# Where the selection's bias is added to the sparse attention scores: on TensorE or on VectorE

## The chip, the cores and the metric

The kernel runs on one core of a Trainium2 chip. A core has five engines that work side by side, each through its own queue in order: TensorE (PE in the profile, its weight loads PEld), VectorE (DVE), ScalarE (ACT), GpSimd (POOL) and SyncE (SP), which here issues the transfers. Matrix products land in PSUM, eight banks of 128 x 512 floats; everything else lives in SBUF. The metric is the device time of one execution in microseconds (us), smaller being better; the time given is the median of the runs.

## What is computed

One block of a streaming encoder over 256 frames of width 1024: a norm, one projection, two attention branches (A: latent attention, B: sparse attention), their gated merge, a projection, and then a mixture of 32 experts. The change touches branch B alone. For every query it scores all admissible keys with a small indexer, keeps the best 64, and attends to those only:

```python
logits = jnp.einsum('bqhd,bkd->bqhk', qii, k_idx).astype(jnp.float32) * (IDX_DIM ** -0.5)
score = jnp.einsum('bqh,bqhk->bqk', wi.astype(jnp.float32), jax.nn.relu(logits))
score = jnp.where(adm[None], score, -jnp.inf)
_, sel = lax.top_k(score, top_k)
sel_ok = (sel // CHUNK) <= q_chunk[None, :, None]
k_sel = gather(k, sel)
v_sel = gather(v, sel)
s = jnp.einsum('bqhd,bqkhd->bhqk', qi, k_sel).astype(jnp.float32) * (DSA_HEAD_DIM ** -0.5)
s = jnp.where(sel_ok[:, None], s, NEG)
p = jax.nn.softmax(s, axis=-1).astype(v.dtype)
return jnp.einsum('bhqk,bqkhd->bqhd', p, v_sel)
```

There are 8 heads of 64 channels, and the 256 queries are two blocks of 128.

## The kernel before, in words

The kernel gathers nothing. `select(j)` (lines 477 to 499) works out the indexer's scores of query block `j`, marks the 64 largest of each row, and writes `bias`, a table of 128 queries by 128 (`j`=0) or 256 (`j`=1) keys: 0 at a chosen key and -1e30 elsewhere (line 499). The attention then runs over all keys of the block, with that bias added to the scores before the softmax, so that keys that are not chosen get weight zero.

`attend_pairs(quad, ...)` (lines 610 to 664) does this for four heads, as a generator that is stepped by hand (lines 727 to 731): first both query blocks of quad 0, then both of quad 1, then the two closing steps. One *round* is one query block `j` of one quad; there are four. A round takes two PSUM banks `p[0]`, `p[1]` from a pool of two (`pss`), two heads in each. It then does, in this order:

- on TensorE, for each bank, one product of the identity with `bias` that opens the bank's sum (line 621, 256 columns for `j`=0 and 512 for `j`=1, full array);
- on TensorE, twelve products of queries and keys (`mm3_pair`, line 318): 32-bit numbers are split into a high and a low part, so each score takes three products, and the two banks use the two halves of the array's rows in turn. They add onto the bias;
- on VectorE, per bank, the negated maximum of each row and head (line 632), read from PSUM;
- on ScalarE, per head, the exponential of scores plus that number with its row sum (line 638), read from PSUM and written to the SBUF tile `P`;
- on VectorE the reciprocal of the sums and the scaling of `P` (lines 641, 643);
- on TensorE the transposes of `P` (line 649), on ScalarE their copy to `PT` (lines 651, 653).

After a quad's two rounds, 16 products with the values (line 661) and a split of the result into high and low (lines 291, 294) give `obT`. It is an operand of the third group of output projections.

Work around it. `project_late` (lines 734 to 746) multiplies the normed input with the gates' weights and the attention results with their output weights. Each 128 x 512 piece of weight is split by `split_late` into a high part on ScalarE (line 282, or 297 where a gain is applied) and a low part on VectorE (line 283, or 297), into four buffers `halves` used in turn, and then feeds six products of 512 columns on TensorE (`mm3`, lines 301 to 303). These pieces need nothing from the sparse attention until `obT`, and TensorE works on them between the steps of the rounds; on ScalarE and VectorE the splits stand in the same queues as the rounds' work. The order on each engine is fixed when the program is built, by a scheduler that simulates the program with priorities (the attention's steps have a raised one, line 667). Weights come through a ring of four SBUF places and other places as they fall free; SP issues a load when the place's last reader is done (`issue`, line 215). From line 930 on TensorE's order is written out by hand: the last projection, the routing, and the experts (`gate_up` line 1056, `down` line 1097), whose weights stream in through the same places.

The lines that matter most below: 621 (identity products), 318 (score products), 632 (row maximum), 638 (exponential), 643 (scaling), 649 (transposes), 301 to 303 (projection products), 282, 283 and 297 (splits), 215 (loads), 1056 (first expert products).

Of the kernel before, what the change touches and what calls it, by code (L numbers as in the profile page):

```python
# [10 lines left out]
F32 = mybir.dt.float32  # L11
F32R = mybir.dt.float32r
I32 = mybir.dt.int32
AF = mybir.ActivationFunctionType
ALU = mybir.AluOpType
AX = mybir.AxisListType
# [62 lines left out]
def block_kernel(ctx: ExitStack, tc: tile.TileContext, a, out, cap=CAP):  # L79
    nc = tc.nc  # L80
# [4 lines left out]
    wk = ctx.enter_context(tc.tile_pool(name="wk", bufs=2))  # L85
# [4 lines left out]
    def after(i, j):  # L90
        tc.add_manual_dep(i.ins, j.ins.name, nosync, reason="the latter goes first")
# [15 lines left out]
    def at(place, shape, dt=F32R, name="r"):  # L107
        n = int(np.prod(shape[1:]))
        t = rp.tile([128, 2048], dt, tag=place,
                    name=name)  # L110
        return shaped(t[:, :n], shape)
# [6 lines left out]
    def pt(name="t", which=None):  # L118

        if which is None:  # L120
            which = t_turn[0] = 1 - t_turn[0]
        return psT.tile([128, 512], F32, tag=f"t{which}", name=name)

    def pss(name="s"):
        return psS.tile([128, 512], F32, tag="s", name=name)

    def bc(ap, n, axis=1):

        p, m = ap.shape
        return ap[:, None, :].to_broadcast([p, n, m]) if axis == 1 else ap[:, :, None].to_broadcast([p, m, n])  # L130
# [37 lines left out]
    ident_r = cp.tile([128, 128], F32R, name="ident_r")  # L168
# [121 lines left out]
    def evac(hi, lo, ps, place=None):  # L290
        i = nc.scalar.copy(hi, ps)
        if place:
            first[place] = i.ins
        return i, nc.vector.tensor_sub(lo, ps, hi.bitcast(F32))
# [17 lines left out]
    row_halves = slice(0, 64), slice(64, 128)  # L312

    def mm3_pair(both, start, stop, behind=None):

        for l, r, s0, s1 in ((1, 3, start, False), (1, 4, False, False), (2, 3, False, stop)):
            for ops in both:
                i = nc.tensor.matmul(ops[0], ops[l], ops[r], start=s0, stop=s1)  # L318
                if behind:
                    after(i, behind)  # L320
                behind = i
        return behind
# [116 lines left out]
    bias = wk.tile([128, 2, 256], F32R, tag="b3", name="bias", bufs=1)  # L439
# [168 lines left out]
    paired = []  # L608

    def attend_pairs(quad, v, oT, op):  # L610


        turn[0] = 1 - turn[0]
        place = f"T{turn[0]}"
        PT = at(place, [128, 4, 3, 128], F32)
        for j in range(2):
            nk = 128 * (j + 1)
            qs = slice(j * 128, (j + 1) * 128)
            p = [pss()[:, :2 * nk] for _ in range(2)]
            for z in range(2):  # L620
                i_ = nc.tensor.matmul(p[z].rearrange("p (h k) -> p h k", h=2), ident_r, bc(bias[:, j, :nk], 2), start=True,
                                      stop=False)
                if not z and paired:
                    after(i_, paired.pop())
            for i in range(2):
                h = 2 * quad + i
                i_ = mm3_pair([(p[z][:, i * nk:(i + 1) * nk], qbT[r, 0, h, qs], qbT[r, 1, h, qs], kbT[r, 0, h, :nk],
                           kbT[r, 1, h, :nk]) for z, r in enumerate(row_halves)], False, i == 1, i_)
            paired.append(i_)
            for z in range(2):  # L630
                nm = wk.tile([128, 4], F32, tag="nm", name="nm")[:, :2]
                nc.vector.tensor_reduce(nm, p[z].rearrange("p (h k) -> p h k", h=2), axis=AX.X, op=ALU.max, negate=True)
                if j or not z:
                    P = wk.tile([128, 512], F32, tag="b2", name="P", bufs=3)
                Pz = P[:, 256 * z:256 * z + 256] if j == 0 else P
                sm = wk.tile([128, 4], F32, tag="sm", name="sm")[:, :2]
                for i in range(2):
                    nc.scalar.activation(Pz[:, i * nk:(i + 1) * nk], p[z][:, i * nk:(i + 1) * nk], AF.Exp,
                                         bias=nm[:, i:i + 1], scale=1.0, accum_out=sm[:, i:i + 1])
                rs = wk.tile([128, 4], F32, tag="rs", name="rs")[:, :2]  # L640
                nc.vector.reciprocal(rs, sm)
                for i in range(2):
                    nc.vector.tensor_scalar(Pz[:, i * nk:(i + 1) * nk], Pz[:, i * nk:(i + 1) * nk], rs[:, i:i + 1], None,
                                            op0=ALU.mult)
                if z == 0 or j:
                    tp = pt()
                for b in range(2 * (j + 1)):
                    c = 256 * z + 128 * b if j == 0 else 128 * b
                    nc.tensor.transpose(tp[:, c:c + 128], P[:, c:c + 128], ident)  # L649
                if j:  # L650
                    nc.scalar.copy(PT[:, 2 * z:2 * z + 2, 1:3], tp.rearrange("p (h b q) -> p h b q", h=2, b=2))
                elif z:
                    first[place] = nc.scalar.copy(PT[:, :, 0], tp.rearrange("p (h q) -> p h q", h=4)).ins
            yield
        o = pss("o")
        for c in range(2):
            for b in range(2):
                for i in range(2):
                    r = slice(64 * i, 64 * i + 64)
                    h = 2 * quad + 4 * c + i  # L660
                    nc.tensor.matmul(o[r, c * 256 + 128 * b:(c + 1) * 256], v[:, b, 64 * h:64 * h + 64],  # L661
                                     PT[:, 2 * c + i, 0:2] if b == 0 else PT[:, 2 * c + i, 2], start=b == 0, stop=b == 1)
        evac(oT[:, 0, quad::2], oT[:, 1, quad::2], o.rearrange("p (c q) -> p c q", c=2), op)
        yield
# [58 lines left out]
    kbT = at("C1", [128, 2, 4, S])  # L723
    dsa_heads(acc, kbT, 0, "C1")
    steps(A[1], 1)
    obT = at("C1", [128, 2, 4, S])
    B = [attend_pairs(quad, vb, obT, "C1") for quad in range(2)]
    steps(B[0], 2)
    steps(B[1], 2)
# [451 lines left out]
    with in_order, tc.manual_schedule(engines={mybir.EngineType.Activation, mybir.EngineType.DVE}):  # L1181
        for grp in range(NG):
# [26 lines left out]
            if grp + 1 < NG:  # L1209
                for c in range(2):  # L1210
                    p = pss("gx")
# [128 lines left out]
```

## Time and profile before

| | us |
|---|---|
| median of 3 runs | 423.73 (422.84 to 423.84) |
| the profiled execution | 422.87 |
| its span, first to last instruction | 421.10 |
| TensorE busy | 391.6 (93%) |
| TensorE weight loads busy | 287.8 (68%) |
| VectorE busy | 205.3 (49%) |
| ScalarE busy | 184.1 (44%) |
| data moved | 135.00 MB, mean 321 GB/s |

How to read it: the profiled execution is 0.86 us below the median of the runs, and 1.77 us of it lie outside the span. Times of instructions are from the span's start. The duration of a product in the trace covers its way through the array; the next one starts long before it ends, so what a product costs TensorE is the distance from its start to the next start. Shares of busy time are averages over stages with different limits: attention and projections to about 204 us, routing to 218, experts from there on.

### The profile page before, as it was taken

How to read it: one execution, taken by the hardware profiler on the slowest of the kernel's cores; microseconds unless marked ns; L12 is line 12 of the kernel's file. 1: busy time of each engine (PE TensorE's matmuls, PEld its weight loads, DVE VectorE, ACT ScalarE, POOL GpSimd, SP SyncE). 2: the span in 40 equal slices, each digit the busy share in tenths (PEclk: the TensorE clock that was granted, in tenths of full speed). 3: DMA queues.
4: the chain of work that ended last, by engine and by line, in shares of the span. 5: the costliest groups of instructions: out<-in, count | busy, mean ns of one | idle time of the engine just before them, and what ended most of it. 6: DMA issues, size and time to landing. Idle time of an engine off the chain costs nothing.

```text
span 421.1 us, 8166 instructions
## 1 busy us (share of the span) xinstructions
PE 391.6 (93%) x3288; PEld 287.8 (68%) x3288; DVE 205.3 (49%) x546; ACT 184.1 (44%) x403; POOL 27.0 (6%) x30
## 2 busy tenths in 40 slices
PE   6999999999999999999999999999999788688880
PEld 3888888888867877888886857575767363364540
DVE  2889689989858665866571212121303021020033
ACT  4876588578857765575442122122122111121143
POOL 0880000000000000000000010101010001000000
PEclk9999999999999999999999999999999996998996
DMA  7995673748544489679867999999999999999962
GB/s 251 401 362 210 244 297 127 264 158 354 199 159 160 184 297 349 229 291 360 319 253 285 422 421 420 421 419 419 418 420 420 421 418 420 421 420 419 415 251 105
DMA packets 20639, 135.00 MB, mean 321 GB/s; under 512 B 2418, under 2 KB 2930, under 8 KB 5620
## 3 DMA queue, kind: packets, MB, share of 16 engines
q1 hardware_dynamic: 20596, 134.42, 80.9%
q8 instruction: 28, 0.46, 0.4%
q14 instruction: 15, 0.12, 0.1%
HBM read 133.36 MB, written 1.05 MB: 319 GB/s over the span
## 4 chain that ended last, share of the span: by engine, by line
PE 75%; DMA 20%; DVE 2%; ACT 1%; issue 0%; SPq 0%; DVEq 0%; ACTq 0%
DMA w<-in_w_moe 19%; PE a L301 13%; PE a L302 13%; PE a L303 13%; PE G L1056 9%; PE gx L904 5%; PE Y L1097 5%; PE OA L1111 3%; PE G L1072 3%; PE s L318 2%; DMA w<-in_w_att 1%; PE o L603 1%; PE t L543 1%; PE t L649 1%; PE o L661 1%; PE t L455 1%
## 5 line engine op out<-in xcount | busy, mean ns | idle before, releaser
L302 PE MATMUL a<-r 128*128 128x512 f32 (+1 forms) x244 | 93.7, 387 | 0.0
L303 PE MATMUL a<-r 128*128 128x512 f32 (+1 forms) x244 | 92.2, 383 | 0.0
L301 PE MATMUL a<-r 128*128 128x512 f32 (+1 forms) x244 | 84.0, 386 | 1.1 <-ACT r L297 1.0
L1056 PE MATMUL G<-w,tok 128*32 128x256 f32 x1024 | 68.5, 394 | 12.1 <-DMA w<-in_w_moe 12.1
L297 DVE SCALAR_TENSOR_TENSOR r<-w,ident,r 128x512 fp32r<-128x512 f32 (+2 forms) x79 | 62.5, 806 | 14.7 <-ACT r L297 14.5
L297 ACT ACTIVATE r<-w,ident 128x512 fp32r<-128x512 f32 (+2 forms) x79 | 56.8, 751 | 24.5 <-PE a L303 22.5
L1056 PEld LDWEIGHTS G<-w,tok 128*32 128x32 f32 x1024 | 29.2, 111 | 37.8 <-issue 14.0
L301 PEld LDWEIGHTS a<-r 128*128 128x128 f32 x244 | 45.0, 188 | 10.4 <-ACT r L297 1.5
L302 PEld LDWEIGHTS a<-r 128*128 128x128 f32 x244 | 45.9, 188 | 8.7 <-DVE r L297 0.5
L303 PEld LDWEIGHTS a<-r 128*128 128x128 f32 x244 | 45.8, 188 | 8.4 <-issue 0.2
L1078 DVE TENSOR_TENSOR P<-G,P 128x64 f32<-128x64 f32 x32 | 7.2, 225 | 78.7 <-ACT P L1077 78.7
L1077 ACT ACTIVATE P<-G 128x64 f32<-128x64 f32 x32 | 7.2, 224 | 70.5 <-PE G L1072 70.5
L1097 PE MATMUL Y<-w,P 128*32 128x256 f32 x512 | 31.0, 382 | 3.2 <-DMA w<-in_w_moe 3.2
L1062 ACT COPY Gs<-G 128x256 f32<-128x256 f32 x32 | 11.9, 372 | 50.1 <-PE G L1056 50.1
L297 DVE SCALAR_TENSOR_TENSOR ysb<-Y,ws,ysb 128x512 fp32r<-128x512 f32 (+1 forms) x18 | 12.5, 692 | 41.2 <-PE OA L1111 21.5
L904 PEld LDWEIGHTS gx<-Pr,x 128*128 128x128 f32 x256 | 29.2, 192 | 3.3 <-issue 2.9
L904 PE MATMUL gx<-Pr,x 128*128 128x128 f32 x256 | 30.7, 278 | 0.2 <-DVE Pr L889 0.2
L283 DVE TENSOR_TENSOR r<-w,r 128x512 fp32r<-128x512 f32 x32 | 21.9, 690 | 14.9 <-ACT r L282 13.2
L889 POOL TENSOR_SCALAR Pr<-P,r 128x128 f32<-128x128 f32 x14 | 8.3, 606 | 316.6 <-PE gx L904 190.8
L282 ACT CAST r<-w 128x512 fp32r<-128x512 f32 x32 | 19.9, 624 | 14.1 <-DVE r L283 7.4
L1097 PEld LDWEIGHTS Y<-w,P 128*32 128x32 f32 x512 | 15.0, 109 | 13.7 <-DMA w<-in_w_moe 3.4
L909 DVE TENSOR_TENSOR tok<-gx,ident 128x512 f32<-128x512 f32 x16 | 11.1, 692 | 27.1 <-PE gx L904 26.9
(223 smaller groups left out, 457.0 us busy)
## 6 DMA issues: line engine op xcount, KB each, us to landing
w<-in_w_moe SPq DMA_DIRECT2D x93, 1024.0 KB, 19.8
w<-in_w_att SPq DMA_DIRECT2D x24, 1024.0 KB, 4.9
w<-in_w_moe SPq DMA_DIRECT2D x6, 512.0 KB, 15.0
w<-in_w_att SPq DMA_DIRECT2D x3, 744.0 KB, 8.2
w<-in_w_att SPq DMA_DIRECT2D x2, 512.0 KB, 5.3
out<-r SPq DMA_DIRECT2D x2, 512.0 KB, 3.6
w<-in_w_att SPq DMA_DIRECT2D x1, 768.0 KB, 5.6
w<-in_w_att SPq DMA_DIRECT2D x2, 372.0 KB, 5.9
```

Of the source, the lines that this page charges most:

```text
L282: nc.scalar.copy(hi, src)
L283: nc.vector.tensor_sub(lo, src, hi.bitcast(F32))
L297: return nc.scalar.mul(hi, ps, g), nc.vector.scalar_tensor_tensor(lo, ps, g, hi.bitcast(F32), op0=ALU.mult, op1=ALU.subtract)
L301: i = nc.tensor.matmul(out_, lh, rh, start=start, stop=False)
L302: nc.tensor.matmul(out_, lh, rl, start=False, stop=False)
L303: nc.tensor.matmul(out_, ll, rh, start=False, stop=stop)
L904: nc.tensor.matmul(p[:, kk * GRP:(kk + 1) * GRP], x2[:, t, k * 128:(k + 1) * 128], Pr[:, t], start=(t == 0 and kk == 0), stop=(t == 1 and ...
L1056: nc.tensor.matmul(G[quarters[2 * z + o], :256], tokens[c][:, kk + o, CAP * e:CAP * e + CAP], w[:, (kk + o) * 512 + z * 256:(kk + o) * 512 ...
L1062: nc.scalar.copy(Gs, G[:, :256])
L1072: nc.tensor.matmul(HT[:, f * 64:(f + 1) * 64], Gs[:, f * 128:(f + 1) * 128], fold, start=True, stop=True)
L1097: nc.tensor.matmul(Y[quarters[e]], hT_[:, e, f], wv[:, f, e], start=f == 0, stop=f == 1)
L1111: nc.tensor.matmul(OA[t][h][:, c0:c0 + w], pl[:, t * 128:(t + 1) * 128], v, start=False, stop=grp == NG - 1 and q0 > 0 and v is lo, skip_g ...
```

## The change

The two products with the identity go. The score products open and close their own sums. VectorE adds the bias while it takes the scores out of PSUM into `P` in SBUF, one addition per bank with the bias repeated for its two heads; the row maximum and the exponentials then read `P`, the exponentials in place. The tile `P` is taken before the addition and not before the exponentials. A round's first score product is ordered behind the last one of the round before, as the first identity product was.

```diff
             p = [pss()[:, :2 * nk] for _ in range(2)]
-            for z in range(2):
-                i_ = nc.tensor.matmul(p[z].rearrange("p (h k) -> p h k", h=2), ident_r, bc(bias[:, j, :nk], 2), start=True,
-                                      stop=False)
-                if not z and paired:
-                    after(i_, paired.pop())
+            i_ = paired.pop() if paired else None
             for i in range(2):
                 h = 2 * quad + i
                 i_ = mm3_pair([(p[z][:, i * nk:(i + 1) * nk], qbT[r, 0, h, qs], qbT[r, 1, h, qs], kbT[r, 0, h, :nk],
-                           kbT[r, 1, h, :nk]) for z, r in enumerate(row_halves)], False, i == 1, i_)
+                           kbT[r, 1, h, :nk]) for z, r in enumerate(row_halves)], True, True, i_)
             paired.append(i_)
             for z in range(2):
-                nm = wk.tile([128, 4], F32, tag="nm", name="nm")[:, :2]
-                nc.vector.tensor_reduce(nm, p[z].rearrange("p (h k) -> p h k", h=2), axis=AX.X, op=ALU.max, negate=True)
                 if j or not z:
                     P = wk.tile([128, 512], F32, tag="b2", name="P", bufs=3)
                 Pz = P[:, 256 * z:256 * z + 256] if j == 0 else P
+                Ph = Pz.rearrange("p (h k) -> p h k", h=2)
+                nc.vector.tensor_add(Ph, p[z].rearrange("p (h k) -> p h k", h=2), bc(bias[:, j, :nk].bitcast(F32), 2))
+                nm = wk.tile([128, 4], F32, tag="nm", name="nm")[:, :2]
+                nc.vector.tensor_reduce(nm, Ph, axis=AX.X, op=ALU.max, negate=True)
                 sm = wk.tile([128, 4], F32, tag="sm", name="sm")[:, :2]
                 for i in range(2):
-                    nc.scalar.activation(Pz[:, i * nk:(i + 1) * nk], p[z][:, i * nk:(i + 1) * nk], AF.Exp,
+                    nc.scalar.activation(Pz[:, i * nk:(i + 1) * nk], Pz[:, i * nk:(i + 1) * nk], AF.Exp,
                                          bias=nm[:, i:i + 1], scale=1.0, accum_out=sm[:, i:i + 1])
```

## Rows read from the trace of the kernel before

**Rows 1.** The page's 40 slices of 10.5 us: busy tenths of TensorE, of DMA.

```profile
PE   6999999999999999999999999999999788688880
DMA  7995673748544489679867999999999999999962
```

**Rows 2.** The page's chain that ended last: shares of the span by engine.

```profile
PE 75%; DMA 20%; DVE 2%; ACT 1%; issue 0%; SPq 0%; DVEq 0%; ACTq 0%
```

**Rows 3.** Stretches of the rounds: busy us and instructions (x) of each engine.

```profile
core 0: us, PE busy (x) PEld busy (x) DVE busy (x) ACT busy (x) POOL busy (x), PEclk, DMA share, GB/s
125.00:131.00 6.00, 6.00 (x43) 4.76 (x41) 4.86 (x14) 2.87 (x11) 0.00 (x0) 1.00 0.40 161
131.00:137.00 6.00, 6.00 (x32) 4.82 (x30) 4.88 (x12) 4.94 (x14) 0.00 (x0) 1.00 0.67 206
143.00:149.00 6.00, 6.00 (x35) 4.53 (x34) 4.74 (x9) 3.81 (x12) 0.00 (x0) 1.00 0.73 239
```

**Rows 4.** The same view around the first expert products.

```profile
219.00:224.50 5.50, 5.50 (x74) 4.05 (x73) 2.50 (x10) 1.21 (x7) 1.21 (x2) 1.00 0.14 24
224.50:320.00 95.50, 95.50 (x1196) 65.17 (x1196) 19.89 (x58) 20.09 (x53) 4.75 (x8) 1.00 1.01 419
```

**Rows 5.** Waits of SP's queue, 212 to 230 us: total, times, longest us.

```profile
SPq L215 <- PE G L1056: 16.3, 5, 11.7
```

**Rows 6.** The identity products by line: ns min/median/max, first and last start, forms.

```profile
L621 PE MATMUL s<-bias,ident_r x8: 277/388/481, 119.3 to 144.3; 128*128 128x256 f32 x4, 128*128 128x512 f32 x4
```

**Rows 7.** TensorE's timeline at four of the eight: start, us, line, form, count.

```profile
119.25 0.38 PE L621 MATMUL s<-bias,ident_r 128*128 128x256 f32 x1
119.56 0.86 PE L603 MATMUL o<-r 128*64 128x256 f32 x6
...
127.46 0.40 PE L621 MATMUL s<-bias,ident_r 128*128 128x512 f32 x1
127.69 0.62 PE L301 MATMUL a<-r 128*128 128x512 f32 x2
...
135.45 0.28 PE L621 MATMUL s<-bias,ident_r 128*128 128x256 f32 x1
135.56 0.40 PE L302 MATMUL a<-r 128*128 128x512 f32 x1
...
144.31 0.48 PE L621 MATMUL s<-bias,ident_r 128*128 128x512 f32 x1
144.72 0.50 PE L318 MATMUL s<-r 64*128 64x256 f32 x3
145.15 0.44 PE L649 MATMUL t<-ident,P 128*128 128x128 f32 x2
145.52 0.86 PE L318 MATMUL s<-r 64*128 64x256 f32 x9
```

**Rows 8.** Groups by line and form: VectorE operations on two tensors (us, mean ns).

```profile
L811 DVE TENSOR_TENSOR x<-a,x 128x512 f32<-128x512 f32 x4 | 2.7, 687 | 1.6 <-PE a L303 1.6
L429 DVE TENSOR_TENSOR m<-r,early 128x256 f32<-128x256 f32 x2 | 0.8, 412 | 0.0
```

**Rows 9.** The same view: ScalarE casts from SBUF (282) and from PSUM (291).

```profile
L282 ACT CAST r<-w 128x512 fp32r<-128x512 f32 x32 | 19.9, 624 | 14.1 <-DVE r L283 7.4 <-PE a L303 6.7
L291 ACT CAST r<-t 128x512 fp32r<-128x512 f32 x12 | 7.0, 585 | 8.3 <-PE t L375 4.2 <-PE t L455 3.0 <-PE t L521 1.1
```

**Rows 10.** ScalarE's longest wait, 119 to 162 us: total, times, longest us.

```profile
ACT r L297 <- PE a L303: 5.7, 7, 2.1
```

**Rows 11.** VectorE's timeline: a split's low part, the last round's scaling.

```profile
142.40 0.69 DVE L283 TENSOR_TENSOR r<-w,r 128x512 fp32r<-128x512 f32 x1 [0.98 <-ACT r L282]
...
149.14 1.12 DVE L643 TENSOR_SCALAR P<-P,rs 128x256 f32<-128x256 f32 x4
```

**Rows 12.** TensorE's timeline: the products of that split, that round's transposes.

```profile
146.31 0.50 PE L301 MATMUL a<-r 128*128 128x512 f32 x1
...
153.47 1.09 PE L649 MATMUL t<-ident,P 128*128 128x128 f32 x8
```

## The prediction

> **What bounds the kernel now.** I read the views from coarse to fine. The page's 40 slices come first [rows 1]: TensorE is busy in nine tenths or more of nearly every slice to about 340 us, while the DMA engines have room until about 230 us and none from there to 400. The chain that ended last says the same in shares: 75% TensorE, 20% DMA, 2% VectorE, 1% ScalarE [rows 2]. So there are two regimes, and the change lies in the first. The stretches in which the four rounds run are next [rows 3]: TensorE is busy 6.00 of 6.00 us in each, VectorE 4.7 to 4.9 of 6, ScalarE 2.9 to 4.9, all at the full granted clock. Busy time of products overstates, since their durations overlap, so I looked at the distances between starts: a projection product of 512 columns follows the one before after 0.23 us (at 127.46 [rows 7]), with no larger holes than the changes of shape. And the other engines wait for TensorE: ScalarE's longest wait in the rounds is for projection products to give a split buffer back, 5.7 us in 7 waits [rows 10]. TensorE's stream of products is the bound there.
>
> The second regime has to pass a gain on. Before it there is a gap: from 219 to 224.5 us the DMA engines are busy only 14%, and from 224.5 on 101% [rows 4]. SP stood in one wait of 11.7 us for the first expert products [rows 5]. Those are at the end of TensorE's chain. The saturated stream therefore starts when TensorE lets it, with the same loads behind it. If TensorE reaches its first expert product earlier by some time, the stream starts and ends earlier by that time: one to one.
>
> **The change part by part.** *Removed: eight identity products*, four of 256 and four of 512 columns [rows 6]. By the undisturbed ones, a product of 512 columns takes 0.23 us of TensorE's stream (127.46 to 127.69) and one of 256 takes 0.11 (135.45 to 135.56) [rows 7]. Together 4 x 0.23 + 4 x 0.11 = 1.36 us, all on the path. If the whole distance to the next start went for each, it would be more: 0.31 at the first, 0.41 at the last of the eight [rows 7], 2.2 us in sum over all eight. But part of that is the change of array shape: after 144.31 come products on half the rows, and where transposes stand before such products (145.15 to 145.52, 0.37 us for two) there is about 0.1 us beside the two transposes, at 0.14 each at most (eight in 1.09 us [rows 12]). That switch stays, with something else ahead of it. Only the product at 119.25 stands between products on 64 columns of the array and brings two switches of its own; taking it out should give some 0.2 us more. So 1.36 to 2.2 us, and I take 1.36 + 0.2 = 1.5 us, near the lower end, since the lower end comes from plain distances. The eight weight loads run beside other products and count nothing.
>
> *Added: eight additions on VectorE*, from PSUM and SBUF into SBUF. The nearest rows are the residual's addition, 687 ns for 512 columns, also from PSUM and SBUF, and 412 ns for a product of 256 columns [rows 8]: 4 x 0.69 + 4 x 0.41 = 4.4 us of VectorE. I take none of it on the path. What hides it is the lead of the splits: the low part that was made from 142.40 to 143.09 [rows 11] feeds products that start at 146.31 [rows 12], by counting the pieces in program order. That is 3.2 us, and four buffers are in turn. A round puts at most 1.4 us (two additions of 512) in VectorE's queue ahead of the next split. If that cover were gone, all 4.4 us would be on the path; both ends stay in the range. Behind each addition stand the row maximum, the scaling and the splits, and for the splits waits TensorE.
>
> *Moved: the row maximum and sixteen exponentials read SBUF.* No row shows a maximum from SBUF; an addition with one operand in PSUM at 687 ns and a split's subtraction wholly in SBUF at 0.69 [rows 8, 11] make the place indifferent to VectorE, so nothing. For ScalarE a cast of 512 columns takes 624 ns from SBUF and 585 from PSUM [rows 9], 0.04 us: at most 16 x 0.04 = 0.6 us over four rounds, and nothing at the least. ScalarE has 1.06 us or more idle in each 6 us [rows 3], so zero on the path.
>
> *The chain of a round grows* by up to two additions, 1.4 us, before its last exponential. Who waits at its end is the last round: its scaling is done at 150.26 [rows 11], its transposes start at 153.47 [rows 12], so 3.2 us lie open. In return the PSUM banks come free after the additions and not after the exponentials, which lets the next round begin earlier; TensorE didn't wait for it, so zero. The tile `P` is taken about 1.4 us earlier; three buffers for at most two in use by a round cover that.
>
> Sum: 1.5 us less. Profiled execution: 422.87 - 1.5 = 421.4, span 421.10 - 1.5 = 419.6. Against the median of the runs, which lies 0.86 above the profiled execution: 423.73 - 1.5 = 422.2.
>
> A rule speaks against all this. The Trainium skill (Perfetto Trace Analysis, Identifying the Most-Contended Engine) says that busy time of matmuls is a poor measure of how close TensorE is to its limit, and that weight-load busy time is a better one. By that measure TensorE has a fifth of its time left in the rounds (4.5 to 4.8 of 6 us [rows 3]), and the removed products would lie in slack, worth 0 and not 1.5 us. The distances between starts disagree here: they leave no holes. It is among the rivals as no change.
>
> **The rivals.** *Something else takes the place of the removed products, no change, 423.7 us.* The program is scheduled anew, each round's scores now come out through one more step on VectorE, and products that were ready in the old order may not be in the new one. It takes only 1.5 us of holes in the 85 us of TensorE's stream from the first identity product, at 119 us [rows 6], to the end of the projections, or one late step at the end of the rounds. For it: VectorE reaches 81% in the rounds (4.88 of 6 [rows 3]), and with 2.2 us of additions in each 12 us it comes near full. Against: the 3.2 us of lead, and other engines that wait for TensorE. Two other forms end at the same time: the stream of weights doesn't start earlier, against which stands the 14% gap [rows 4, 5]; or TensorE has slack in the rounds that busy time hides, against which stand the distances between starts [rows 7].
>
> *VectorE becomes the bound of the rounds, slower.* If a round's additions, maxima and scalings come in one block ahead of the splits, the lead of 3.2 us is used up, and from there on each us on VectorE is one on TensorE. The additions alone put 1.4 us there, so this decides from 1.8 us of other delay in one round, at one of the two 256-key rounds. If all 4.4 us came through: 4.4 - 1.4 = 3.0 us slower, 426.7. For it speaks the load from 125 to 137 us: 9.7 of 12 us busy [rows 3] plus 2.2 added. Against it, VectorE has idle time right after each round in which it can make the lead good.
>
> *All distances go with the products,* and the earlier free banks let the rounds close up: 2.2 us less, 421.5. This is the forecast's own upper end.
>
> **How the numbers follow.** Forecast (1.0 to 2.7 us less, likeliest 1.5): 0.6. No change (within about 1 us): 0.28, of it 0.05 for slack in TensorE and 0.03 for the stream of weights. VectorE the bound, or an order that is worse in another way: 0.12. A measurement of this kernel can tell about 0.3%, 1.27 us, from no change: faster means below 422.46, slower above 425.0. Some of the forecast's cases fall short of that bound (a gain of 1.0 to 1.27) and I give them a tenth of its chance: faster 0.54, slower 0.10, same 0.36. The range has to leave out no more than 0.2: below, 423.73 - 2.7 = 421.0; above, it goes past no change and takes in the first part of the slower case, 424.4.
>
> **What would show it.** Line 621 gone, and the DMA gap that ended at 224.5 us [rows 4] ending some 1.5 us earlier, with a saturated stream as long as before (right size, right passing on). Eight additions of about 0.69 and 0.41 us on the new line, and TensorE still 6.00 of 6 in every stretch (right cover). Wrong: holes between projection products after a round, with ScalarE's or VectorE's split as the releaser (VectorE the bound); or a shorter time to 204 us and an unchanged end (the gain lost in the stream).

## The result: 0.67% faster, nearly twice the gain that was forecast

| | before | after |
|---|---|---|
| median of 4 runs each, us | 423.42 | 420.69 (420.53 to 421.01) |
| the profiled execution, us | 422.87 | 420.53 |
| its span, us | 421.1 | 418.7 |
| TensorE reaches the first expert product at, us | 221.81 | 219.75 |

The ratio is 0.9933, with a 95% interval of 0.9915 to 0.9951. The forecast was 1.5 us less; the medians fell by 2.7 us and the profiled execution by 2.3. The sign and the way were right, the size was not: 420.69 us is below the low end of the range, 421.0.

**Where the gain arises.** The stretch to look at is TensorE's stream from the last transposes of the indexer's keys, ahead of everything that the change touches, to the first expert product behind it. Its two ends in the timeline (start, duration, line, form, count), first before, then after:

```profile
83.78 1.05 PE L543 MATMUL t<-ident,r 128*96 128x128 f32 x8
...
221.81 2.80 PE L1056 MATMUL G<-w,tok 128*32 128x256 f32 x48
```

```profile
83.86 1.05 PE L543 MATMUL t<-ident,r 128*96 128x128 f32 x8
...
219.75 2.80 PE L1054 MATMUL G<-w,tok 128*32 128x256 f32 x48
```

From 83.78 to 221.81 us are 138.03 us before, from 83.86 to 219.75 are 135.89 after. The difference, 2.14 us, is the gain in TensorE's stream. This distance, called *the stream* below, is the finer of the two measures for every run here: the times of the kernel before scatter by 1.0 us over four runs and by 2.8 us over 26, and the stream of a second profile of the changed kernel was 135.86 us.

**How it is passed on.** After's two stretches that answer to [rows 4]:

```profile
core 0: us, PE busy (x) PEld busy (x) DVE busy (x) ACT busy (x) POOL busy (x), PEclk, DMA share, GB/s
216.00:222.50 6.50, 6.50 (x81) 5.02 (x81) 3.36 (x16) 1.47 (x7) 1.20 (x2) 1.00 0.09 16
222.50:318.00 95.50, 95.50 (x1196) 65.17 (x1196) 19.90 (x58) 20.09 (x53) 4.73 (x8) 1.00 1.01 419
```

The gap in the transfers ends 2 us earlier, and the saturated stretch holds the same 1196 products in the same 95.5 us. The last product of the kernel starts at 408.29 us instead of 410.29: the gain goes through to the end, one to one.

**The cover.** After's stretches of the rounds, beside [rows 3]:

```profile
core 0: us, PE busy (x) PEld busy (x) DVE busy (x) ACT busy (x) POOL busy (x), PEclk, DMA share, GB/s
125.00:131.00 6.00, 6.00 (x45) 4.59 (x44) 5.95 (x17) 3.60 (x11) 0.00 (x0) 1.00 0.29 122
131.00:137.00 6.00, 6.00 (x36) 4.71 (x34) 6.00 (x17) 5.85 (x21) 0.00 (x0) 1.00 0.59 190
137.00:143.00 6.00, 6.00 (x35) 5.07 (x33) 5.67 (x16) 5.40 (x14) 0.00 (x0) 1.00 0.89 347
143.00:149.00 6.00, 6.00 (x41) 4.57 (x40) 4.93 (x10) 4.10 (x9) 0.00 (x0) 1.00 0.88 336
```

TensorE is busy throughout, at the full granted clock. VectorE, 17.75 us busy of the 24 before, is now at 22.55: 4.1 us of additions, and the rounds lie closer together. The scores of the last round start at 136.12 us, where they started at 144.72 [rows 7]. Part of the 17.75 is a stretch of before that [rows 3] leaves out:

```profile
137.00:143.00 6.00, 6.00 (x38) 5.14 (x39) 3.26 (x10) 5.10 (x16) 0.00 (x0) 1.00 0.35 146
```

**The new operations.** The groups by line and form, 118 to 160 us (busy us, mean ns, idle time before):

```profile
L631 DVE TENSOR_TENSOR P<-s,bias 128x512 f32<-128x512 f32 x4 | 2.6, 679 | 0.0
L633 DVE TENSOR_REDUCE nm<-P 128x2 f32<-128x512 f32 x4 | 2.5, 677 | 0.0
L633 DVE TENSOR_REDUCE nm<-P 128x2 f32<-128x256 f32 x4 | 1.5, 407 | 0.0
L631 DVE TENSOR_TENSOR P<-s,bias 128x256 f32<-128x256 f32 x4 | 1.5, 418 | 0.7 <-PE s L318 0.7
L636 ACT ACTIVATE P<-P,nm 128x256 f32<-128x256 f32 x8 | 4.0, 505 | 0.0
L636 ACT ACTIVATE P<-P,nm 128x128 f32<-128x128 f32 x8 | 3.1, 391 | 0.0
```

The additions take 679 and 418 ns, for 687 and 412 assumed [rows 8]. The row maximum takes 677 and 407 ns from SBUF, where it took 682 and 418 from PSUM. An exponential takes 505 and 391 ns, where it took 470 and 374, so all 16 take 0.4 us more.

### The profile page after: what moved, and what is told of

Its sections match the earlier page's. It is cut to its first block, busy times and chain, and to the rows that moved or that the text cites. A ratio compares the mean times of both kernels' runs of the same rounds, so it can differ in the third digit from the quotient of the medians.

```text
span 418.7 us, 8153 instructions
## 1 busy us (share of the span) xinstructions
PE 390.6 (93%) x3280; PEld 286.7 (68%) x3280; DVE 208.2 (50%) x554; ACT 184.4 (44%) x403; POOL 27.0 (6%) x30
## 4 chain that ended last, share of the span: by engine, by line
PE 75%; DMA 20%; DVE 2%; ACT 1%; issue 0%; SPq 0%; DVEq 0%; ACTq 0%
DMA w<-in_w_moe 19%; PE a L301 13%; PE a L302 13%; PE a L303 13%; PE G L1054 9%; PE gx L902 5%; PE Y L1095 5%; PE OA L1109 3%; PE G L1070 3%; PE s L318 2%; DMA w<-in_w_att 1%; PE t L543 1%; PE t L455 1%; PE o L603 1%; PE o L659 1%; PE t L647 1%
## 5 line engine op out<-in xcount | busy, mean ns | idle before, releaser
L1054 PE MATMUL G<-w,tok 128*32 128x256 f32 x1024 | 69.6, 399 | 14.0 <-DMA w<-in_w_moe 14.0
L1060 ACT COPY Gs<-G 128x256 f32<-128x256 f32 x32 | 11.9, 372 | 48.4 <-PE G L1054 48.4
L283 DVE TENSOR_TENSOR r<-w,r 128x512 fp32r<-128x512 f32 x32 | 21.9, 690 | 13.2 <-ACT r L282 10.2
L1070 PEld LDWEIGHTS G<-cst,Gs 128*128 128x128 f32 x128 | 17.5, 199 | 9.8 <-issue 5.3
```

Source lines behind the costliest of these rows:

```text
L283: nc.vector.tensor_sub(lo, src, hi.bitcast(F32))
L1054: nc.tensor.matmul(G[quarters[2 * z + o], :256], tokens[c][:, kk + o, CAP * e:CAP * e + CAP], w[:, (kk + o) * 512 + z * 256:(kk + o) * 512 ...
L1060: nc.scalar.copy(Gs, G[:, :256])
L1070: nc.tensor.matmul(HT[:, f * 64:(f + 1) * 64], Gs[:, f * 128:(f + 1) * 128], fold, start=True, stop=True)
```

## The experiments

The theory, formed on the two traces: 2.1 us is what the eight products took of TensorE's stream, but they are worth very different amounts. Look at the first, at 119.25 us [rows 7], with what stands around it, before:

```profile
118.68 0.65 PE L603 MATMUL o<-r 128*64 128x256 f32 x2
119.25 0.38 PE L621 MATMUL s<-bias,ident_r 128*128 128x256 f32 x1
119.56 0.86 PE L603 MATMUL o<-r 128*64 128x256 f32 x6
120.36 0.66 PE L455 MATMUL t<-ident,r 128*128 128x128 f32 x4
```

and after:

```profile
118.77 0.87 PE L603 MATMUL o<-r 128*64 128x256 f32 x8
119.57 0.66 PE L455 MATMUL t<-ident,r 128*128 128x128 f32 x4
```

Line 603 holds branch A's products with the values, eight for a quad, of which four stand here; each shows as two instructions. (So it is at line 661: eight products and sixteen instructions for a quad, not sixteen products.) They use 64 columns of the array, the left and the right half in turn. After, the trace has them in step: each instruction of a left product starts 6 or 7 ns before one of the right product, and all eight are done with in 0.80 us (118.77 to 119.57). Before, the identity product stands between the first product and its partner. The first runs alone (118.68 to 119.25, 0.57 us), the identity product takes 0.31, and the six instructions that are left run one product out of step (a 256-column instruction beside a 128-column one) and take 0.80 by themselves: 1.68 us in all (118.68 to 120.36). So this one product cost 0.88 us. By 0.11 and 0.23 us each, the other seven make 3 x 0.11 + 4 x 0.23 = 1.25, and the sum is 2.13 us. The rival: the product cost the predicted 0.3 us, and the rest came from somewhere else, such as the new order of the program.

### The product taken out of the pair (before, one order added)

```diff
+                    last_value.append(nc.tensor.matmul(o[r, c * 256 + 128 * b:(c + 1) * 256], v[:, b, 64 * (4 * quad + h):][:, :64],
+                                     PT[:, h, 0:2] if b == 0 else PT[:, h, 2], start=b == 0, stop=b == 1))
...
                 if not z and paired:
                     after(i_, paired.pop())
+                elif not z:
+                    after(i_, last_value[-1])
```

All eight identity products stay; the first is ordered behind branch A's last value product.

> The kernel before, with one order added: the first identity product may start only behind branch A's last value product, so it no longer stands between two of them; TensorE's order is otherwise the same. Theory A (that one product breaks the side-by-side running of the value products on the two column halves, and costs 0.88 us where 0.12 are its own columns): the first expert product starts 0.75 us earlier than before, at about 221.1 instead of 221.8, and the time falls by about 0.75 us. Rival B (what the change gave beyond the columns comes from banks that fall free earlier and rounds that close up): 0.2 us at most, for two changes of array shape.

Ratio 0.9978 [0.9963, 0.9993]; stream 137.16 us (84.08 to 221.24), 0.87 less than before, where theory A had 0.75. The same place in its timeline:

```profile
118.99 0.87 PE L604 MATMUL o<-r 128*64 128x256 f32 x8
119.79 0.66 PE L455 MATMUL t<-ident,r 128*128 128x128 f32 x4
...
121.30 0.87 PE L604 MATMUL o<-r 128*64 128x256 f32 x8
122.10 0.39 PE L622 MATMUL s<-bias,ident_r 128*128 128x256 f32 x1
122.33 0.60 PE L455 MATMUL t<-ident,r 128*128 128x128 f32 x4
122.86 0.50 PE L301 MATMUL a<-r 128*128 128x512 f32 x1
```

The eight instructions are in step again, 0.80 us. The moved product takes 0.23 us in its new place (122.10 to 122.33), but a hole of as much behind the four transposes goes with it: from their start to the next product were 0.76 us before and are 0.53 here. (In the trace of before, that hole is a wait for a cast: the weight load ahead of the projection product stands 0.3 us for line 291 on ScalarE.) So the gain is nearly the whole 0.88, and the price of the moved product itself is not to be had from this run. The rival is out: two fifths of the change's gain come from the place of one product, with nothing removed.

### One dummy product put into the pair (after, one product added)

```diff
+                    if quad == 1 and (c, b, i) == (0, 0, 0):
+                        early_bank.append(pss())
+                        between.append(nc.tensor.matmul(early_bank[0][:, :256].rearrange("p (h k) -> p h k", h=2), ident_r,
+                                                        bc(bias[:, 0, :128], 2), start=True, stop=True))
+                        after(between[0], i_)
```

Its result is not used; the round's scores overwrite it.

> The changed kernel, with one identity product of 256 columns put back between the first two of branch A's last value products; nothing reads it, it only stands there. TensorE's order is otherwise the same. Theory A: the first expert product starts 0.88 us later than in the changed kernel, at 220.6 instead of 219.75. Price by columns and two changes of shape, as the prediction had it: 0.3 us, 220.05. Rival B: the same 0.3, since banks and rounds are as in the changed kernel.

Ratio 0.9958 [0.9944, 0.9972]; stream 136.74 us (85.88 to 222.62), 0.85 more than after. The first expert product stands at 222.62 and not at the expected 220.6 us because the profiled execution was the longest of five (423.78 us; the median is 422.07) and came to the key transposes 2.0 us later, ahead of all that is compared here. The timeline has the pattern of before again:

```profile
120.79 0.65 PE L604 MATMUL o<-r 128*64 128x256 f32 x2
121.36 0.39 PE L610 MATMUL s<-bias,ident_r 128*128 128x256 f32 x1
121.68 0.86 PE L604 MATMUL o<-r 128*64 128x256 f32 x6
122.47 0.65 PE L455 MATMUL t<-ident,r 128*128 128x128 f32 x4
```

1.68 us, as before. Taken out of the one kernel or put into the other, the product is worth 0.85 to 0.88 us in this place.

### Half of the change at a time

VectorE adds the bias in the rounds of 256 keys alone, or of 128 keys alone; the other rounds keep the identity products (`on_pe` is `j == 0` in the first kernel, `j == 1` in the second).

```diff
+            on_pe = j == 0
+            for z in range(2 if on_pe else 0):
+                k_ = nc.tensor.matmul(p[z].rearrange("p (h k) -> p h k", h=2), ident_r, bc(bias[:, j, :nk], 2), start=True, stop=False)
...
+                src = p[z].rearrange("p (h k) -> p h k", h=2) if on_pe else Ph
+                if not on_pe:
+                    nc.vector.tensor_add(Ph, p[z].rearrange("p (h k) -> p h k", h=2), bc(bias[:, j, :nk].bitcast(F32), 2))
```

> One part of the change alone: VectorE adds the bias in the two rounds of 256 keys (four banks of 512 columns), TensorE keeps the identity products in the rounds of 128 keys, the one between the value products among them. Theory A: 4 x 0.23 = 0.92 us less TensorE, first expert product at 220.9. Rival B (earlier banks in the long rounds do it): most of the whole gain, first expert product near 220.0. VectorE the bound: 221.8 or later.

> The other part alone: VectorE adds the bias in the two rounds of 128 keys (four banks of 256 columns), TensorE keeps its four products of 512 columns. Theory A: 0.88 + 3 x 0.11 = 1.2 us less TensorE, first expert product at 220.6, so the smaller products are worth more than the larger ones. By columns and two changes of shape: 0.44 + 0.2 = 0.64 us, 221.2.

Both expectations failed. With 256 keys alone the ratio is 1.0005 [0.9992, 1.0018] and the stream 138.45 us, 0.42 longer than before where it should have been 0.92 shorter. With 128 keys alone it is 1.0013 [0.9992, 1.0035] and 138.21 us, 0.18 longer instead of 1.2 shorter. Half of the change gives nothing, though each kernel has four identity products less. The first kernel reaches the first expert product at 222.18 us, where its expectation had VectorE as the bound (221.8 or later); but TensorE has no wait in its trace between 84 and 212 us. Its score products in the 256-key rounds show what happened instead:

```profile
127.48 0.38 PE L318 MATMUL s<-r 64*128 64x256 f32 x1
...
128.67 0.98 PE L318 MATMUL s<-r 64*128 64x256 f32 x11
...
141.53 0.38 PE L318 MATMUL s<-r 64*128 64x256 f32 x1
...
143.66 0.73 PE L318 MATMUL s<-r 64*128 64x256 f32 x7
...
144.91 0.50 PE L318 MATMUL s<-r 64*128 64x256 f32 x4
```

Twelve products that could run together are split into 1 and 11, and 1, 7 and 4; before it was 12, and 3 and 9. The program's order is made anew for every edit, and its order of ready work doesn't keep such a group whole. I counted how often TensorE's stream leaves the products on the whole array for products on half its rows (scores) or half its columns (values), from the key transposes to the expert products: 12 times before and after, 15 and 14 in these two kernels. In the second kernel there is also a wait of 0.34 us for a split at 130.82. The distances from each start to the next, summed by kind of product over the stream, account for the first kernel: 1.29 us of identity products are gone, but projection products take 1.01 more, score products 0.49, value products 0.14 and transposes 0.06. A new theory follows: each such *trip* costs about 0.3 us, and the order decides how many there are.

### Groups kept whole (the change, and the kernel before)

The first value product of a quad waits for the last copy to `PT`, and the first score product of a round for the last reader of its two banks, so that a group that starts can run through. This adds dependencies and removes no work.

```diff
+                    if (c, b, i) == (0, 0, 0):
+                        tc.add_manual_dep(i_.ins, last.ins.name, full, reason="a group starts whole")
...
+                if ready:
+                    tc.add_manual_dep(i.ins, ready.ins.name, full, reason="a group starts whole")
```

> The changed kernel with one rule more: a group of products on part of the array (the value products of four heads, the score products of a round) may start only when all that it needs is there, so that it runs whole. TensorE leaves the full array 12 times before the experts in place of 16, with the same products. Theory A' (beside its columns, each such excursion costs TensorE about 0.38 us): 4 x 0.38 = 1.5 us less than the changed kernel, 134.4 us from the key heads' transposes to the first expert product, 419.2 us. Columns alone: no change, 135.9.

> The kernel before, identity products and all, with the same rule that a group starts whole: 13 excursions in place of 16, and no identity product between value products. Theory A': three excursions and the broken pairing less, about 3 x 0.38 + 0.5 = 1.6 us faster than before, 136.4 us to the first expert product. Against the changed kernel under the same rule (12 excursions) it is then 1.36 + 0.38 = 1.7 us longer: the columns of the identity products and one excursion. If the gain of the change were in something other than columns and shapes, the two would differ by more than 2 us or by nothing.

(The expectations count four more trips in each of these kernels than the count above; the differences are the same.) On the changed kernel: ratio 0.9910 [0.9881, 0.9938] against before, stream 134.67 us (84.61 to 219.28), 1.22 less than the change alone. The trips fall from 12 to 8, so one is worth 0.3 us, with all that the new order changed along with it. On the kernel before: ratio 0.9962 [0.9947, 0.9977], stream 136.70 us, 1.33 less, with 9 trips. Both gained somewhat less than expected, and both have the sign. In the changed kernel branch A's value products now run in one group:

```profile
119.97 1.52 PE L609 MATMUL o<-r 128*64 128x256 f32 x16
121.42 0.66 PE L459 MATMUL t<-ident,r 128*128 128x128 f32 x4
```

16 instructions in 1.45 us, where after has two groups of 0.80 each, and other products between them. With whole groups on both sides the change is worth 136.70 - 134.67 = 2.03 us, where 1.7 was expected; the expectation had named more than 2 us as a sign of something else than columns and shapes. No identity product stands inside a value group there, so the sum above does not apply: by plain distances, with that product at 0.11, it would be 1.36 us. The rest is in the distances of the identity products themselves. All of them stand directly ahead of a round's scores there; two of the four places:

```profile
123.18 0.40 PE L625 MATMUL s<-bias,ident_r 128*128 128x256 f32 x2
123.50 0.89 PE L319 MATMUL s<-r 64*128 64x128 f32 x12
...
127.06 0.72 PE L625 MATMUL s<-bias,ident_r 128*128 128x512 f32 x2
127.71 0.98 PE L319 MATMUL s<-r 64*128 64x256 f32 x12
```

The eight take 0.32 + 0.65 here and 0.42 + 0.64 in the other two places, 2.03 us in all, 0.67 above the plain 1.36. Without them, projection products and transposes take 0.22 us more, and score products 0.20 less (one trip less, 8 for 9). So the 2.03 us are accounted for by columns and changes of product kind; of the 0.67 us beyond the plain price, only a third came back elsewhere.

### VectorE's cover, tested by more additions

One more addition of the bias on each bank in the first kernel, three more in the second. The second and further additions only push the keys that are out further down.

```diff
                 nc.vector.tensor_add(Ph, p[z].rearrange("p (h k) -> p h k", h=2), bc(bias[:, j, :nk].bitcast(F32), 2))
+                for _ in range(3):
+                    nc.vector.tensor_add(Ph, Ph, bc(bias[:, j, :nk].bitcast(F32), 2))
```

> The changed kernel with each of the eight additions done twice, which adds 4.4 us to VectorE and nothing to TensorE; TensorE's order has as many changes of array shape as in the changed kernel. Theory A (the additions lie beside TensorE's stream, and there is cover left): the distance from the key heads' transposes to the first expert product stays within 0.3 us of the changed kernel's 135.9 us, and the time too. Rival C (VectorE is at its limit between 125 and 143 us in the changed kernel, 5.7 to 6.0 of 6 us busy): up to 4.4 us longer.

> The changed kernel with each of the eight additions done four times: 13.2 us more on VectorE, nothing on TensorE, which has as many changes of array shape as in the changed kernel. It looks for the point from which VectorE decides. Theory A: cover of some 10 us over the rounds (VectorE's idle time between 119 and 162 us), so 2 to 6 us longer than the changed kernel, with TensorE waiting for splits. Rival C: 8 to 13 us longer.

With 4.4 us more on VectorE: ratio 0.9944 [0.9924, 0.9965], stream 136.50 us, 0.61 longer than after, twice the bound that was expected. The list of TensorE's waits is empty for it, but one round was held: of the twelve score products from 129.50 us the first starts alone and the second 0.27 us later, at 129.77, when VectorE has just ended (129.72) the two additions that empty the two banks, which fits a wait for the second bank; the group takes 1.15 us, where after's takes 0.89. A second score product stands alone at 141.51. By kind, score products take 0.56 us more than in after, projection products 0.48 (they start again behind products of another kind at five more places, at about 0.09 us each), transposes 0.28 less and value products 0.15 less: for the most part, the order was made anew once more. With 13.2 us more: ratio 1.0035 [1.0021, 1.0050], stream 140.14 us, 4.25 longer than after. VectorE is now at 6.00 of 6 in every stretch from 125 to 155 us, and TensorE waits. One of those stretches and the first in which TensorE has holes, and then all of TensorE's waits from 84 to 212 us (total, times, longest us):

```profile
149.00:155.00 6.00, 6.00 (x32) 4.67 (x32) 6.00 (x12) 3.77 (x7) 0.00 (x0) 1.00 0.92 352
155.00:162.00 7.00, 6.27 (x38) 4.45 (x34) 7.00 (x18) 6.12 (x18) 0.00 (x0) 1.00 0.78 301
```

```profile
PE t L649 <- ACT r L297: 0.7, 1, 0.7
PE a L301 <- ACT r L291: 0.7, 1, 0.7
PE a L301 <- ACT r L297: 0.6, 1, 0.6
PE a L302 <- DVE r L297: 0.3, 1, 0.3
```

The waits are for splits and casts, as the rival that makes VectorE the bound has it, and they sum to 2.3 us; the other 1.95 us of the 4.25 have no wait in this list, and whether the order alone made them wasn't followed up. So the change's 4.1 us are covered; twice as much costs TensorE about a quarter of a microsecond at one place; four times as much is not covered.

### The change and the whole groups side by side

The changed kernel and the one with whole groups once more, on one chip, in five rounds.

> The changed kernel as it is, beside the next run on one chip. Theory A: 2.1 us of TensorE's stream less than before, passed on whole, and so a ratio of 0.993 to 0.995 to the kernel before.

> The changed kernel in which groups on part of the array start whole, timed beside the changed kernel on one chip. Theory A' (the 1.2 us that TensorE's stream was shorter in the trace are passed on whole): 1.2 us, 0.3%, less than the changed kernel; ratio to the kernel before 0.990 to 0.992. If the stream of weights doesn't start earlier for it: the same time as the changed kernel.

The change: 0.9935 [0.9920, 0.9951], median 420.79 us, stream 135.86. With whole groups: 0.9910 [0.9893, 0.9926], median 419.98 us, stream 134.67. Against the kernel before both are faster. Between the two, the intervals overlap slightly (0.9920 to 0.9926); the streams, 134.67 twice against 135.89 and 135.86, carry the verdict for whole groups. It is the fastest version here.

## Why the forecast was right in kind and too small

**Bound and passing on: right.** TensorE's stream was the bound, and 2.14 us of it came out as 2.0 us at the last product. The rule that weighed against the change (the Trainium skill, Perfetto Trace Analysis, Identifying the Most-Contended Engine) would have put the removed products into slack, on weight loads of 4.5 to 4.8 us in 6. The runs don't agree with that use of it here: one product moved, with no work taken away, made the stream 0.87 us shorter. The distances between starts were the better guide, though the reading of them missed one hole larger than a change of shape, the wait for a cast behind the transposes at 122.67 us.

**The removed products: the term that failed.** The step was "Only the product at 119.25 stands between products on 64 columns of the array and brings two switches of its own; taking it out should give some 0.2 us more". The place was seen, the cost was taken from the wrong thing. What it cost were not two switches but its neighbours' running side by side: 0.88 us instead of 0.11 + 0.2 = 0.31. The distances to be read were not those of the product (0.31 us to the next start), but those of the whole group around it: 1.68 us for eight instructions and the product. The second group of eight on the same line takes 0.80 us in the trace of before as well (121.87 to 122.67), so the comparison could have been made before the result:

```profile
121.87 0.87 PE L603 MATMUL o<-r 128*64 128x256 f32 x8
122.67 0.66 PE L455 MATMUL t<-ident,r 128*128 128x128 f32 x4
```

The other seven stand in the forecast at their plain 1.25 us, and 0.88 + 1.25 = 2.13 us meets the 2.14 measured. The 0.88 is shown by two runs; the 1.25 was not measured by itself, and that the sum meets so well is in part chance. By kind, identity products take 2.22 us less in the change, value products 0.42, transposes 0.37 and score products 0.07 less, and projection products 0.95 more: the sum is right, but the new order moved about 1 us from some kinds to others. And "That switch stays, with something else ahead of it" held only in part: in the pair with whole groups, where no value group is broken, the products were worth 1.8 us (2.03 less the 0.20 of the split score group) and not the plain 1.36.

With 2.13 us in place of 1.5, the forecast's own sum gives 423.73 - 2.13 = 421.6 us, inside the range. The 0.9 us from there to 420.69 are not in the stream: 0.3 is the start (423.73 was the median of three runs, and with the fourth it is 423.42), and 0.6 is what the medians fell beyond the stream, 2.73 us for 2.14. The profiled execution fell by 2.34. Behind the last product, the trace of after is 0.4 us shorter (from VectorE's last operation to the end of the span 5.86 us before, 5.46 after), but the second profile of the changed kernel has 5.84 there, so that is scatter. In the later five rounds the medians differ by 2.60 us. The intervals of both ratios (2.1 to 3.6 and 2.1 to 3.4 us) still hold the 2.14; where more than that would come from, no trace here shows.

**The range's low end** took the sum of all distances, 2.2 us, and 0.5 more. Beyond the 2.13 it left 0.6 us, where the start and the medians' further fall took 0.9.

**Cover: right, and thinner than it was drawn.** The additions cost 4.1 us of VectorE and no wait of TensorE. From 125 to 137 us VectorE came out as full as the forecast had it (9.7 + 2.2 = 11.9 of 12 us; 5.95 + 6.00 measured). What it left out is that the rounds close up and keep VectorE as busy for another 6 us (5.67 from 137 to 143). In the same stretch of before, which its rows left out, VectorE was busy 3.26 us and ScalarE 5.10, so "1.06 us or more idle" was 0.90 there. With 8 us of additions in the four rounds VectorE seems to begin to hold TensorE (0.27 us at one place), and with 17 it decides.

**Reading from SBUF: right.** The maximum is indifferent to the place within 11 ns; the exponentials cost 0.4 us, for 0.6 at most.

**The rivals.** "No change" named a new order, with holes, as its way. It didn't take the gain here, but the halves of the change show that the way was real, less by holes (one wait of 0.34 us) than by more trips: there it took 1.34 and 1.38 us, all of the expected gain and more. 0.28 was no exaggerated chance for it. "All distances go" came nearest, at 421.5 us. Its 2.2 us didn't allow for the 0.57 us that lay hidden in one group, nor for the time that came back in projection products; in the pair with whole groups, where there is no such group, it came close: 2.03 us of distances went, 0.22 came back, and the split score group made that good.

## What to carry to other kernels

Before you price a TensorE instruction by the distance to the next start, look at what stands on both sides of it: if these are products on halves of the array that could run side by side, the price is the time of the whole group with it, less that of the same group without it. Elsewhere the price lay between the plain distances (1.36 us for the eight here) and the whole distances to the next start (2.03), at about 1.8. Count how often the stream goes between whole-array and half-array products; where a scheduler orders the stream, keeping such groups whole may bring about half as much as the removal of real work (1.22 us beside 2.14 here). And don't expect two halves of an edit to add up where every edit remakes the order: measure the stretch of the stream, and count its trips.

## What the runs showed of the chip beyond that

A trip away from the whole array costs about 0.3 us here (1.22 us for four), at a granted clock of 1.00. Single changes show in the distances: a score product that stands alone costs 0.26 us (122.47 to the next start at 122.73 in after's timeline), and the first projection product behind it 0.33 (122.73 to 123.06), where 0.23 is usual [rows 7]. Behind four transposes, the first takes 0.32 (119.98 to 120.30):

```profile
119.98 0.48 PE L302 MATMUL a<-r 128*128 128x512 f32 x1
120.30 0.39 PE L303 MATMUL a<-r 128*128 128x512 f32 x1
...
122.47 0.32 PE L318 MATMUL s<-r 64*128 64x128 f32 x1
122.73 0.50 PE L301 MATMUL a<-r 128*128 128x512 f32 x1
123.06 0.40 PE L302 MATMUL a<-r 128*128 128x512 f32 x1
```

The Trainium skill (TensorEngine Tiling (Array Packing), Key Properties) says that changing the tiling mode drains TensorE, with no figure. These rows fit that, at about 0.1 us for a change, but don't single it out: transposes use the whole array too, and the product behind them takes nearly as much more. So about 0.1 us goes with a change from scores or transposes to projection products, and what makes it stays open.
